# Down projections in another order of products, and the next norm's operands made step by step

## The chip, the cores and the metric

The kernel runs on one core of a Trainium2 chip. The metric is device time in microseconds, from launch to end, as the median of several runs. The kernel before takes 1988.11 us (three runs, 1987.03 to 1989.14). All times of single instructions come from one further, profiled execution.

## The reference

The reference is a decoder trunk of two layers on x of 512 tokens by 1024 channels, in float32. Each layer is

```
x += 1/2 * SwiGLU_1(RMSNorm(x))
x += W_out( g_pool * P_pool(PoolMixer) + g_attn * P_attn(SWA-GQA with sinks) )
x += 1/2 * SwiGLU_2(RMSNorm(x))
```

with

```python
def rmsnorm(x, g):
    y = xf * lax.rsqrt(jnp.mean(xf * xf, axis=-1, keepdims=True) + EPS)
    return y * g
def swiglu(h, w_gu, w_down):            # w_gu 1024 x 5632, w_down 2816 x 1024
    g, u = jnp.split(h @ w_gu, 2, axis=-1)
    return (jax.nn.silu(g) * u) @ w_down
```

The middle line, called mix below, has a pooling branch and a windowed attention branch on one norm. The change touches its end alone. There are four SwiGLU stages (called ffn), two mix stages, and the order is ffn, mix, ffn, ffn, mix, ffn.

## The kernel before

**Precision.** Every large matrix product is computed in three matmuls. An operand is split into a high part in fp32r, which ScalarE makes by a cast, and a low part, which VectorE makes by subtracting the high part from the operand (`split`, lines 148 to 161). Then high x high, high x low and low x high are added up in PSUM.

**Fewer products.** In an ffn, gate/up and down are done in the form of Strassen and Winograd: operand and weight are cut into 2 x 2 blocks, and seven products of sums of blocks take the place of eight. The seven products are named a11, s1, s2, a12, s3, s4 and a22. Each runs through `strassen` (line 526) as two chunks of weights, c = 0 and 1. A chunk is one tile of 128 x 1024 (smaller where the width is 384), and takes two quarters (q = 0 and 1) of six matmuls each: 24 matmuls a product. The results accumulate in pairs of PSUM banks, three of which have roles: a11, s2, s3 and a22 share pair A, s1 and s4 share pair C, and a12 has pair D. Within a pair the later product is added to the earlier one, so that between them an engine must have read the sum that is needed (`steps[kind]`), and the first matmul of the later product waits for that read. A and D change roles after each seven. A fourth pair, `turn`, takes transposes.

**Stages of an ffn.** The inner width of 2816 is done in three groups, of 2 x 384, 2 x 512 and 2 x 512 columns (the first ffn begins with the 384, the others have 512, 384, 512). A group is two `block` calls (gate and up for one half of its columns each, 384 or 512 wide) and one `down`, which multiplies the result with its rows of the down weights and adds it into x. After a block, `turned` transposes its results r and p with PE and makes operands of the down from them: the result t = 1 (p) at once, the result t = 0 (r) when `flush` is called later. `made` splits an operand into one of three tiles `op`, whose numbers are in AT (line 32): a name may reuse a tile only when the product that read it is done. f["a"], f["b"] and f["c"] are float tiles from which the operands s1, s2, a22, s3 and s4 come.

**Weights.** `Weights` holds a plan of all chunks in the order of use and a list of loads. A load goes by SP's DMA queue into one of seven raw tiles; where the chunk is a sum of two weight blocks (s1, s3), a second, accumulating DMA follows on POOL's queue. The chunks of s2 and s4 are not loaded: VectorE adds s2 from a11 and s1, and s4 from s2 and a12 (`add_up`). `prep` (line 288) is called once per chunk and looks ahead: low parts two chunks ahead, high parts three, sums four. A raw tile is free when its high part, its low part and its sum, if it has one, are made; only then is the next load issued. The sums lie in tiles of the pool `sums`, which is open only within an ffn (`open_sums`; W.sums is None outside).

**Order of the work.** All engines run in the order in which the program is written (`InOrder`, line 91, whose line 99 is the line that the profile shows for every instruction). Work beside the products is put in by hand: `steps` after a product, `mid` after a quarter of a product, and `pend`, a list of which `due` takes the first.

**The next norm.** While the last down of an ffn still adds into x, `feed(q, i, bank)` (line 374) transposes a part of x: token half i, channels of quarter q. ScalarE scales it by the norm's gain, and it is split. For a mix this is all. For an ffn (`halves`), feeds give the blocks B11, B12, B21 and B22, and combinations of them give the operands T1 = B11 - B12, T3 = B22 - B12, T2 (from B11 and T3) and T4 (from T2 and B21); j = 0, 1 are the two halves of each. Before, feed computes a combination as soon as its last block is there. The quarters (2, 0) and (3, 0) can only be fed after the last product's addition, and run in the next stage's first product. At the end of mix (lines 1118 to 1158) the same feeds run between the output products. `sums` of the norm (line 462) turns the sums of squares into rstd, in a chain of short VectorE instructions; the Silu after a12 needs it.

The order of products before is

```python
ORDER = ("a11", "s1", "s2", "a12", "s3", "s4", "a22")   # blocks
DOWN  = ("a11", "s1", "s2", "a12", "s4", "s3", "a22")   # downs
FIRST = ("a11", "s1", "a12", "s2", "s3", "s4", "a22")   # the first such block of an ffn
```

## Time and profile before

| what | value |
|---|---|
| median of three runs | 1988.11 us |
| the profiled execution: time | 1990.38 us |
| its span, first to last instruction | 1988.4 us |
| PE (TensorE) busy | 1885.0 us, 95% |
| DVE (VectorE) busy | 1453.1 us, 73% |
| ACT (ScalarE) busy | 1010.1 us, 51% |
| POOL (GpSimd) busy | 124.9 us, 6% |
| granted TensorE clock, mean | 0.989 |
| DMA | 292.80 MB, mean 147 GB/s |

The profile gives for each engine its busy time, for each instruction its start and length, and the idle time of its engine ahead of it with the engine and tile that ended it ("<-"). Tiles have the program's names: mm for PSUM pairs, wh and wl for high and low parts of weights, raw for loaded weights, sums for added ones, op for operands of a down, xgh, xgl and more for operands of a norm. A view of the timeline gives start, length, engine, line, operation, tiles and shapes, a count where equal instructions follow each other, and the wait in brackets. A view of stretches gives busy times between two moments.

### The profile page before, as it was taken

What the parts mean: (1) busy time and instruction counts of PE and PEld (TensorE: products, weight loads), DVE (VectorE), ACT (ScalarE), POOL (GpSimd) and SP (SyncE); (2) the same over time, 40 slices, a digit from 0 to 9 for tenths busy, and PEclk for the clock granted to TensorE, in tenths of its full rate; (3) what the DMA queues carried; (4) which work ended last, traced back from release to release, by engine and by line L of the source; (5) the groups of instructions that cost most, each with busy time, mean ns of one, the idle gap of its engine ahead of it and who ended that gap; (6) DMA issues with size and microseconds to landing.
All of it is one profiled execution on the core that took longest, in us unless ns stands there. A gap on an engine that the chain in (4) does not pass through costs nothing.

```text
span 1988.4 us, 23898 instructions
## 1 busy us (share of the span) xinstructions
PE 1885.0 (95%) x8928; PEld 1566.8 (79%) x8928; DVE 1453.1 (73%) x1829; ACT 1010.1 (51%) x1493; POOL 124.9 (6%) x152
## 2 busy tenths in 40 slices
PE   9999999899998899999879999998999998999998
PEld 8778787787787788878658797877877876889786
DVE  7877878567555787878767878785765647878777
ACT  6545455545435554545555454555454455545453
POOL 0100000000000000100000011000000000001100
PEclk9999999999999999999989999999999999999999
DMA  7776675322232766776546576753222236667763
GB/s 238 185 201 180 179 192 139 110 85 74 75 113 57 198 164 159 172 213 169 148 116 174 143 193 188 186 148 118 84 70 85 96 75 177 170 159 178 210 172 95
DMA packets 87571, 292.80 MB, mean 147 GB/s; under 512 B 9856, under 2 KB 10112, under 8 KB 87456
## 3 DMA queue, kind: packets, MB, share of 16 engines
q1 hardware_dynamic: 67104, 223.47, 33.8%
q0 software_dynamic: 20208, 67.78, 20.5%
q8 instruction: 70, 1.15, 0.2%
q14 instruction: 45, 0.37, 0.1%
q10 hardware_dynamic: 144, 0.03, 0.0%
HBM read 289.15 MB, written 2.10 MB: 146 GB/s over the span
## 4 chain that ended last, share of the span: by engine, by line
PE 71%; DVE 18%; ACT 6%; issue 3%; DMA 1%; SPq 0%; DVEq 0%; ACTq 0%; POOLq 0%
PE mm L99 65%; DVE wl L99 5%; DVE x L99 3%; PE sc L99 3%; DVE sums L99 2%; DVE op L99 2%; ACT wh L99 1%; DVE fa L99 1%; PE pt L99 1%; ACT xgh L99 1%; PE pt_pv L99 1%; DMA raw<-in_w_g 1%; ACT xg L99 1%; ACT more L99 1%; DVE t L99 1%
## 5 line engine op out<-in xcount | busy, mean ns | idle before, releaser
L99 ACT CAST wh<-raw 128x1024 fp32r<-128x1024 f32 (+3 forms) x443 | 434.2, 987 | 320.5 <-PE mm L99 244.8
L99 DVE TENSOR_TENSOR wl<-raw,wh 128x1024 fp32r<-128x1024 f32 (+3 forms) x443 | 505.6, 1145 | 119.9 <-PE mm L99 60.7
L99 PE MATMUL mm<-wh,op 128*128 128x512 f32 x1232 | 399.1, 399 | 35.5 <-DVE x L99 26.2
L99 PE MATMUL mm<-wh,more 128*128 128x512 f32 (+1 forms) x1104 | 338.0, 377 | 10.4 <-ACT u L99 10.4
L99 PE MATMUL mm<-wl,xgh 128*128 128x512 f32 (+2 forms) x840 | 312.9, 372 | 15.3 <-DVE wl L99 15.2
L99 PE MATMUL mm<-wh,xgh 128*128 128x512 f32 (+2 forms) x840 | 314.4, 374 | 0.1
L99 PE MATMUL mm<-wh,xgl 128*128 128x512 f32 (+2 forms) x840 | 311.5, 371 | 0.0
L99 PEld LDWEIGHTS mm<-wh,op 128*128 128x128 f32 x1232 | 233.3, 190 | 91.7 <-ACT wh L99 14.4
L99 PE MATMUL mm<-wl,op 128*128 128x512 f32 x616 | 245.8, 399 | 18.4 <-DVE wl L99 18.4
L99 PEld LDWEIGHTS mm<-wh,more 128*128 128x128 f32 x1104 | 208.0, 190 | 42.9 <-ACT u L99 12.0
L99 ACT CAST wh<-sums 128x1024 fp32r<-128x1024 f32 (+1 forms) x140 | 137.4, 982 | 161.7 <-DVE sums L99 142.7
L99 PE MATMUL mm<-wl,more 128*128 128x512 f32 (+1 forms) x552 | 208.5, 378 | 4.2 <-DVE wl L99 4.2
L99 PEld LDWEIGHTS mm<-wl,xgh 128*128 128x128 f32 x840 | 159.3, 190 | 40.6 <-DVE wl L99 19.6
L99 DVE TENSOR_TENSOR wl<-sums,wh 128x1024 fp32r<-128x1024 f32 (+1 forms) x140 | 156.7, 1135 | 41.8 <-ACT wh L99 22.0
L99 PEld LDWEIGHTS mm<-wh,xgl 128*128 128x128 f32 x840 | 159.3, 190 | 21.6
L99 PEld LDWEIGHTS mm<-wh,xgh 128*128 128x128 f32 x840 | 159.2, 189 | 21.4 <-ACT wh L99 0.4
L99 POOL DMA_DIRECT2D raw<-in_w_g x92 | 79.5, 864 | 1415.0 <-DMA raw<-in_w_g 662.9
L99 PEld LDWEIGHTS mm<-wl,op 128*128 128x128 f32 x616 | 117.3, 190 | 52.4 <-DVE wl L99 29.7
L99 PE MATMUL mm<-xgh,wh 128*128 128x512 f32 x320 | 129.5, 405 | 0.0
L99 PE MATMUL mm<-xgh,wl 128*128 128x512 f32 x320 | 125.2, 391 | 0.0
L99 PE MATMUL mm<-xgl,wh 128*128 128x512 f32 x320 | 125.0, 391 | 0.0
L99 DVE SCALAR_TENSOR_TENSOR x<-mm,x 128x1024 f32<-128x1024 f32 (+1 forms) x96 | 103.1, 1084 | 26.2 <-PE mm L99 26.2
(246 smaller groups left out, 2405.6 us busy)
## 6 DMA issues: line engine op xcount, KB each, us to landing
raw<-in_w_g SPq DMA_DIRECT2D x160, 512.0 KB, 4.5
raw<-in_w_d SPq DMA_DIRECT2D x100, 512.0 KB, 4.5
raw<-in_w_g POOLq DMA_DIRECT2D x64, 512.0 KB, 5.5
raw<-in_w_g SPq DMA_DIRECT2D x77, 384.0 KB, 3.9
raw<-in_w_d POOLq DMA_DIRECT2D x40, 512.0 KB, 5.5
raw<-in_w_gate SPq DMA_DIRECT2D x32, 512.0 KB, 3.3
raw<-in_w_g POOLq DMA_DIRECT2D x28, 384.0 KB, 5.1
raw<-in_w_br SPq DMA_DIRECT2D x16, 512.0 KB, 3.3
```

The costliest lines, as they stand in the source:

```text
L99: return lambda *args, **kw: self.tc.keep_in_program_order(call(*args, **kw))
```

## The change

- DOWN becomes a11, s1, s2, s4, s3, a12, a22, and the operand tiles get new numbers. f["b"] is finished after a11, the operand s4 is made after s1, s3 after s2, a12 in a flush after s4, and a22 after s3.
- FIRST goes away: the first block of an ffn uses ORDER. The order of the loads stays as it was in every block. The sums pool is opened at the start of each ffn but the first, not after a11. rstd is computed after s2, not after s1.
- The combinations become functions of their own: t1, t3 (only the float tile), t2, t3_split and t4. In the last down the feeds of token half 1 run in s3 and a12, those of half 0 in a22, where t3 and t1 also run. In mix, t1 follows its feed, and t3 stands after the last feed, ahead of the last additions into x.
- `left` puts on the list what remains: t2 twice, two feeds, t3_split twice, t4 twice. They run in a11 (t2 after its first quarter, the feeds after its second and third), s1 and s2 of the next ffn. For a mix only the two feeds are on the list.

```diff
-DOWN = ("a11", "s1", "s2", "a12", "s4", "s3", "a22")
-FIRST = ("a11", "s1", "a12", "s2", "s3", "s4", "a22")
+DOWN = ("a11", "s1", "s2", "s4", "s3", "a12", "a22")
...
-AT = {"a11": 0, "s1": 1, "s2": 2, "s3": 0, "a12": 1, "s4": 2, "a22": 1}
+AT = {"a11": 0, "s1": 1, "s2": 2, "s4": 0, "s3": 1, "a12": 2, "a22": 0}
...
-            head = [name[k, c] for k in (("a11", "s1") if order is FIRST else ("s1",)) for c in range(2)]
-            rest = [c for c in self.loads[first:] if not any(c is h for h in head)]
-            self.loads[first:] = head + rest
+            loads = ("a11", "s1") if start else ("s1", "a11")
+            self.loads[first:] = [name[k, c] for k in (*loads, "a12", "s3", "a22") for c in range(2)]
...
                 self.keep[1, j] = scaled(self.place(0, 0, j, F32))
-                d = temp("d")
-                nc.vector.tensor_tensor(out=d, in0=self.keep[0, j], in1=self.keep[1, j], op=ALU.subtract)
-                split(*self.both(T1, j), d)
-            elif i == 1:
-                xg = scaled(temp("xg"))
-                split(*self.both(B22, j), xg)
-                self.keep[2, j] = t = self.place(1, 0, j, F32)
-                nc.vector.tensor_tensor(out=t, in0=xg, in1=self.keep[1, j], op=ALU.subtract)
-                split(*self.both(T3, j), t)
             else:
-                xg, t, u = scaled(temp("xg")), temp("t2"), temp("t4")
-                split(*self.both(B21, j), xg)
-                nc.vector.scalar_tensor_tensor(
-                    out=t, in0=self.keep[0, j], scalar=-1.0, in1=self.keep[2, j], op0=ALU.mult, op1=ALU.subtract
-                )
-                split(*self.both(T2, j), t)
-                nc.vector.scalar_tensor_tensor(out=u, in0=t, scalar=-1.0, in1=xg, op0=ALU.mult, op1=ALU.subtract)
-                split(*self.both(T4, j), u)
+                self.keep[3 - i, j] = scaled(temp("xg"))
+                split(*self.both(B22 if i else B21, j), self.keep[3 - i, j])
+
+        def t1(self, j):
+            d = temp("d")
+            nc.vector.tensor_tensor(out=d, in0=self.keep[0, j], in1=self.keep[1, j], op=ALU.subtract)
+            split(*self.both(T1, j), d)
+
+        def t3(self, j):
+            self.keep[4, j] = t = self.place(1, 2, j, F32)
+            nc.vector.tensor_tensor(out=t, in0=self.keep[2, j], in1=self.keep[1, j], op=ALU.subtract)
+
+        def t2(self, j):
+            t = self.keep[0, j]
+            nc.vector.scalar_tensor_tensor(
+                out=t, in0=t, scalar=-1.0, in1=self.keep[4, j], op0=ALU.mult, op1=ALU.subtract
+            )
+            split(*self.both(T2, j), t)
+
+        def t3_split(self, j):
+            split(*self.both(T3, j), self.keep[4, j])
+
+        def t4(self, j):
+            u = temp("t4")
+            nc.vector.scalar_tensor_tensor(
+                out=u, in0=self.keep[0, j], scalar=-1.0, in1=self.keep[3, j], op0=ALU.mult, op1=ALU.subtract
+            )
+            split(*self.both(T4, j), u)
...
+    def left(nm):
+        last = [(lambda bank, q=q: nm.feed(q, 0, bank)) for q in (2, 3)]
+        if nm.halves:
+            step = lambda f: [(lambda bank, j=j: f(j)) for j in range(2)]
+            last = step(nm.t2) + last + step(nm.t3_split) + step(nm.t4)
+        pend.extend(last)
...
                 nc.scalar.copy(out=tile_["p"], in_=pt)
-                if nm.rstd is None:
-                    nm.sums()
...
                     nc.scalar.copy(out=tile_["u"][:, q, :], in_=pt[:, q, :])
+                if nm.rstd is None:
+                    nm.sums()
...
                 made("s2", f["a"], n)
-                nc.vector.tensor_tensor(out=f["b"], in0=f["c"], in1=f["b"], op=ALU.subtract)
...
-            a11 = add(0, 0, 0.5)
+            def a11(pt):
+                add(0, 0, 0.5)(pt)
+                nc.vector.tensor_tensor(out=f["b"], in0=f["c"], in1=f["b"], op=ALU.subtract)
 
             def s1(pt):
                 add(1, 1, -0.5)(pt)
-                made("s3", f["b"], n)
-                return flush
+                made("s4", f["c"], n)
 
             def s2(pt):
                 add(1, 0, 0.5)(pt)
-                made("s4", f["c"], n)
-
-            def a12(pt):
-                add(0, 0, 0.5)(pt)
-                made("a22", f["a"], n)
-                whole(0, 0)
-
-            def s3(pt):
-                add(1, 1, -0.5)(pt)
-                whole(1, 1)
+                made("s3", f["b"], n)
 
             def s4(pt):
                 add(1, 0, 0.5)(pt)
                 whole(1, 0)
                 if final:
                     W.sums = None
+                return flush
+
+            def s3(pt):
+                add(1, 1, -0.5)(pt)
+                made("a22", f["a"], n)
+                whole(1, 1)
+
+            def a12(pt):
+                add(0, 0, 0.5)(pt)
+                whole(0, 0)
...
-                Dd = roles[2]
-                for i, (kind, q, t) in enumerate((("s4", 0, 0), ("s3", 0, 1), ("a22", 2, 1))):
-                    for k in range(2):
-                        bank = (Dd, turn)[k][:, 0, :]
-                        mid[kind, k, 1] = lambda q=q + k, t=t, bank=bank: nxt.feed(q, t, bank)
-                pend.extend((lambda bank, q=q: nxt.feed(q, 0, bank)) for q in (2, 3))
+                spot = [t[:, 0, :] for t in (turn, roles[2])]
+                feed = lambda q, t, at: lambda: nxt.feed(q, t, spot[at])
+                mid.update({
+                    ("s3", 0, 1): feed(0, 1, 1), ("s3", 1, 1): feed(1, 1, 0), ("a12", 0, 1): feed(2, 1, 0),
+                    ("a12", 1, 1): feed(3, 1, 0), ("a22", 0, 1): feed(0, 0, 0), ("a22", 1, 0): feed(1, 0, 1),
+                })
+                if nxt.halves:
+                    mid["a22", 0, 0] = lambda: [nxt.t3(j) for j in range(2)]
+                    mid["a22", 1, 1] = lambda: [nxt.t1(j) for j in range(2)]
+                left(nxt)
...
+        if nm is not first:
+            open_sums()
...
-                    starts = W.sums is None
                     mid = {}
-                    if nm is first and starts:
-                        mid["s1", 1, 1] = flush
-                    elif starts:
-                        mid = {("a11", k, 1): lambda bank=bank: due(bank[:, 0, :]) for k, bank in ((0, turn), (1, roles[2]))}
-                    block(n, i, FIRST if starts else ORDER, mid)
+                    if nm is first:
+                        if gi == 0:
+                            mid["s1", 1, 1] = flush
+                    elif gi == i == 0:
+                        mid = {("a11", 0, 0): lambda: [due(), due()], ("a11", 0, 1): lambda: due(turn[:, 0, :]),
+                               ("a11", 1, 0): lambda: due(roles[2][:, 0, :])}
+                        mid.update({(kind, c, 1): due for kind in ("s1", "s2") for c in range(2)})
+                    block(n, i, ORDER, mid)
...
                     if d and b % 2:
-                        nxt.feed(*next(feeds), side_bank[b // 2])
+                        q, i = next(feeds)
+                        nxt.feed(q, i, side_bank[b // 2])
+                        if nxt.halves and i:
+                            nxt.t1(q)
...
                     nxt.feed(*next(feeds), side_bank[b])
+        for n in range(2):
+            nxt.t3(n)
         for n in (0, 1):
             added(1, n)
-        pend.extend((lambda bank, q=q: nxt.feed(q, 0, bank)) for q in (2, 3))
+        left(nxt)
```

More of the change, by code (lines that the diff above doesn't have):

```diff
@@ L189, in __init__ @@
                                 src = lambda h, k, c, w=w: w[h, 2 * k + c]
-                                self.block(src, (2 * n, 2 * n), FIRST if 2 * gi + i == int(plain) else ORDER)
+                                self.block(src, (2 * n, 2 * n), ORDER, 2 * gi + i == int(plain))
                         if at:
@@ L204, in add, with block @@
             return c
-        def block(self, w, sizes, order):
+        def block(self, w, sizes, order, start=False):
             name, first = {}, len(self.loads)
@@ L498, in trunk, with due @@
     pend = []
-    def due(bank):
+    def due(bank=None):
         if pend:
             pend.pop(0)(bank)
+    def left(nm):
[4 more added lines that the diff above has]
+        pend.extend(last)
     @with_exitstack
```

## The prediction

> **What bounds the kernel now.** I read the busy times and then PE's waits, because PE is busy 95% of the span and DVE 73%.
>
> ```profile
> PE 1885.0 (95%) x8928; PEld 1566.8 (79%) x8928; DVE 1453.1 (73%) x1829; ACT 1010.1 (51%) x1493; POOL 124.9 (6%) x152
> ...
> PE mm L99 <- DVE wl L99: 37.9, 38, 3.3
> PE mm L99 <- DVE x L99: 28.2, 14, 5.5
> PE mm L99 <- ACT u L99: 10.4, 4, 3.3
> PE mm L99 <- DVE op L99: 9.3, 12, 1.1
> PE pt L99 <- DVE x L99: 8.8, 6, 3.4
> ```
>
> Of the waits: total, count, longest. PE idles some 98 us in all. The second row is mostly a22 waiting until DVE has added s3 into x (same pair), the third s3 waiting for the copies of s2 in the first block of an ffn. The other three are PE waiting for VectorE work that stands in a queue. So I went through the stretches; the columns are length, busy time of PE, PEld, DVE, ACT, POOL, granted clock, DMA share, GB/s.
>
> ```profile
> 234.30:272.40 38.10, 38.10 (x171) 31.50 (x170) 27.34 (x25) 19.77 (x22) 2.81 (x4) 1.00 0.69 186
> 189.70:217.30 27.60, 25.50 (x119) 20.32 (x118) 26.41 (x25) 14.70 (x15) 2.58 (x3) 1.00 0.69 177
> 217.30:234.30 17.00, 15.59 (x69) 12.64 (x68) 11.67 (x11) 5.25 (x5) 0.87 (x1) 1.00 0.58 160
> 189.70:234.30 44.60, 41.09 (x186) 32.96 (x185) 38.08 (x34) 19.95 (x20) 3.45 (x4) 1.00 0.65 170
> 826.40:861.90 35.50, 31.35 (x140) 24.60 (x138) 31.39 (x34) 16.27 (x20) 4.02 (x5) 1.00 0.69 185
> 312.30:369.00 56.70, 49.18 (x226) 38.97 (x225) 43.72 (x43) 32.91 (x53) 1.86 (x3) 0.97 0.43 129
> 1310.20:1368.00 57.80, 50.21 (x227) 39.67 (x226) 43.82 (x43) 33.06 (x54) 1.86 (x3) 0.94 0.43 126
> 620.20:682.20 62.00, 50.19 (x211) 39.38 (x210) 41.49 (x57) 33.08 (x50) 3.45 (x4) 0.94 0.41 113
> 1619.00:1681.40 62.40, 51.95 (x211) 40.55 (x210) 41.49 (x57) 33.12 (x50) 3.45 (x4) 0.92 0.40 111
> 939.90:1052.50 112.60, 91.60 (x386) 72.25 (x385) 81.43 (x95) 58.85 (x88) 6.91 (x8) 0.92 0.49 131
> ```
>
> The first row is a gate/up block without a stall: seven products in 38.1 us, 5.44 each, 2.72 a chunk of twelve matmuls. The fourth is a down of width 512: the same seven products and two rounds of eight transposes (0.9 each) take 44.6, so 4.7 are lost. In its first part DVE is full (26.4 of 27.6), in its last third it is not (11.7 of 17.0). The fifth is a down of width 384. Then come final down to mix (twice), mix to ffn (twice) and final down to ffn, where time is lost and the clock drops.
>
> **The change, part by part. The downs.** There are nine without feeds: five of width 512 (the very last down is one) and four of 384. PE's rows of one, then DVE's:
>
> ```profile
> 190.37 0.47 PE L99 MATMUL mm<-wh,op 128*128 128x512 f32 x1
> 199.25 0.50 PE L99 MATMUL mm<-wl,op 128*128 128x512 f32 x1 [0.21 <-DVE wl L99]
> 201.89 1.04 PE L99 MATMUL pt<-cst,r 128*128 128x128 f32 x8
> 209.46 0.73 PE L99 MATMUL mm<-wh,op 128*128 128x512 f32 x2 [0.59 <-DVE op L99]
> 216.26 0.50 PE L99 MATMUL mm<-wl,op 128*128 128x512 f32 x1 [1.29 <-DVE wl L99]
> 228.62 0.47 PE L99 MATMUL mm<-wh,op 128*128 128x512 f32 x1 [1.41 <-DVE x L99]
> ```
>
> ```profile
> 196.85 1.22 DVE L99 TENSOR_TENSOR fb<-fc,fb 128x1024 f32<-128x1024 f32 x1
> 197.98 1.22 DVE L99 TENSOR_TENSOR wl<-raw,wh 128x1024 fp32r<-128x1024 f32 x1
> 201.39 2.35 DVE L99 TENSOR_TENSOR wl<-sums,wh 128x1024 fp32r<-128x1024 f32 x2
> 207.06 1.22 DVE L99 TENSOR_TENSOR sums<-sums,raw 128x1024 f32<-128x1024 f32 x1
> 227.25 1.23 DVE L99 SCALAR_TENSOR_TENSOR x<-mm,x 128x1024 f32<-128x1024 f32 x1 [1.67 <-PE mm L99]
> ```
>
> One step on DVE takes 1.135 us from start to start. The four waits sum to 3.5; the other 1.2 of the 4.7 is a restart of 0.3 after each. The a22 wait is no backlog: DVE was idle ahead of 227.25. I lay the new order on the same queue; no instruction is added or dropped.
> - fb leaves its place ahead of the low part (wl) at 197.98, which moves to 196.85: the wait of 0.21 goes. fb comes after the addition of a11, so the next low part, the first of s2, still starts at 201.39 and ends at 202.6. The transposes of r (201.89) had hidden that; they now come after s4. a11 and s1 end at 190.37 + 10.9 = 201.3, so s2's second matmul waits 1.1.
> - Behind it stand, 1.135 each: sum for s4 (it stood at 207.06, two products later), low part, sum, addition of s1, low part of operand s4, and then the low part of the first s4 weights, which ends at 209.4. s2 ends at 207.9, so s4 waits 1.35.
> - From there DVE gains: twelve steps to the low part of operand a22 end at about 223.5. PE: s4 ends at 214.7, transposes to 215.6, s3 to 221.0, a12 to 226.5, and a22 starts without a wait. The operand of a12 (218.4) is in time for 221.0.
> a22 then ends at 231.9 instead of 228.62 + 5.44 = 234.06. Two of four waits are left. I take 2.0 (the width 384 walks to the same within 0.2): 9 x 2.0 = **18 us**.
>
> **DMA.** The order of the loads stays. But a12's raw tiles are now freed by their low parts at about 217 and 221, where they were freed at 207 and 212 (sums at 207.06 and one step on), and of seven raw buffers these gate the next block's second s1 load and its first a11 load.
>
> ```profile
> raw<-in_w_g SPq DMA_DIRECT2D x160, 512.0 KB, 4.5
> raw<-in_w_g POOLq DMA_DIRECT2D x64, 512.0 KB, 5.5
> ```
>
> a11 is then issued near 221 and lands near 226 with 4.5, near 229 if it shares the engines with two others; the matmuls that read it start at 232. The s1 tile's second half, on POOL's queue, follows its first and is used 8 us later still. Cost nothing; at 384, where chunks are shorter, up to 0.5 after each of four downs. I book 0.
>
> **The boundaries.** PE's waits in the first ffn (one), from final down to ffn (four), and one each of mix to ffn and of final down to mix; then DVE's queue there and one row of ScalarE's:
>
> ```profile
> 63.46 0.44 PE L99 MATMUL mm<-wh,more 128*128 128x384 f32 x1 [0.95 <-ACT u L99]
> 976.66 0.63 PE L99 MATMUL mm<-cst,x 128*128 128x128 f32 x4 [1.03 <-DVE x L99]
> 985.95 0.80 PE L99 MATMUL mm<-wh,op 128*128 128x512 f32 x1 [5.48 <-DVE x L99]
> 1001.28 0.30 PE L99 MATMUL pt<-cst,x 128*128 128x128 f32 x1 [3.39 <-DVE x L99]
> 1033.03 0.79 PE L99 MATMUL mm<-wh,more 128*128 128x512 f32 x1 [3.33 <-ACT u L99]
> 631.84 0.30 PE L99 MATMUL pt<-cst,x 128*128 128x128 f32 x1 [2.38 <-DVE x L99]
> 356.90 0.79 PE L99 MATMUL mm<-wh,op 128*128 128x512 f32 x1 [4.03 <-DVE x L99]
> ```
>
> ```profile
> 979.59 0.69 DVE L99 TENSOR_TENSOR d<-more 128x512 f32<-128x512 f32 x1 [1.94 <-ACT more L99]
> 980.96 0.69 DVE L99 TENSOR_TENSOR xgl<-d,xgh 128x512 fp32r<-128x512 f32 x1 [0.68 <-ACT xgh L99]
> 984.68 1.22 DVE L99 SCALAR_TENSOR_TENSOR x<-mm,x 128x1024 f32<-128x1024 f32 x1
> 661.21 1.04 ACT L99 CAST wh<-raw 128x1024 fp32r<-128x1024 f32 x1 [1.93 <-DMA raw<-in_w_g]
> ```
>
> A combination costs DVE 2.05 us: 0.69, 0.68 of waiting for ScalarE's cast, 0.69. DVE runs in order, so the addition that a22 needs (984.68) stood behind two of them. I walk each boundary like the down.
> - **Final down to ffn.** Stall-free: 2 x 38.1, 1.8 of transposes for r and p, eight feeds of 0.6 (976.66): 82.8 of 112.6. After the change, counted from the last block's end: waits of 1.1 and 1.4 as above, 0.3 and 0.9 before feeds; a22 ends at 47.0. a11 starts at 48.6, 1.6 late: its pair is the old D, which holds the feed (1, 0) until ScalarE, behind two sums of squares and two casts, has scaled it. DVE has the low part of that feed at 49.9, then both T1, 4.1, then a22's additions, 1.2: 55.1, and the feed in a11, due at 51.3, waits 3.8. DVE goes on: a low part and a sum to 57.3, both T2 to 61.3, the feed's low part to 62.6, and to 63.8 the low part that s1 wants at 61.9: 1.9. Walked on, 1.8 and 0.2 in s3 and s4. In all 13.0. Restarts 9 x 0.3, and 1.5 for the clock after the 3.8: 100.0, 12.6 less. Counting restarts at the 0.13 that the walk of before needs gives 14; I take **13.3**.
> - **Mix to ffn**, twice. Stall-free 45.9 (38.1, two out tiles of 2.7, four feeds) of 62.2. T3's cast and low part leave the queue ahead of x, so 2.38 becomes 2.1 at most; then 0.3. From the additions' end, 11.4 after the start of the stretch, DVE has two low parts and a sum (4.2, with a wait for a cast), both T2 (4.0), the feed (1.4), and s1's low part ends at 22.1; s1 wants it at 18.6: 3.5. Then 0.2, 1.8, 0.2: 8.1. The waits for u go, and 661.21's too, because the sums are open from the start and free a11's raw tiles before a11 runs, not after. With restarts and 1 for the clock 56.4: 5.8 each, **11.6**.
> - **Final down to mix**, twice. 4.03 goes, but B11's counterpart comes later, so mix's first products wait 1.9 in all: 2.0 gained each, and the clock's loss, 1.5 and 2.6 (0.03 x 56.7 and 0.06 x 57.8, less what falls into the waits): **8.1**.
> - First block of the first ffn: its u wait is 0.95 and some returns as a wait for a12's low part: **0.5**. The 14 short instructions for rstd move to s2; Silu of a12, 5.4 us later, covers them.
>
> **The clock.** Where waits are short, as in 189.70:234.30, the granted clock stays 1.00; in the stretches with waits of 2.4 to 5.5 us it is 0.92 to 0.97. [...]
>
> **Sum.** 18 + 13.3 + 11.6 + 8.1 + 0.5 = 51.5 off the span of 1988.4: 1936.9. The profiled execution took 1990.38, 2.0 more than its span, and 2.3 more than the median of 1988.11; against the median that is **1936.6**.
>
> **Rivals.**
> - DVE takes it back: the waits at s2 and s4 grow to what the four were, and the later feeds are exposed. For it: DVE is full in 189.70:217.30, and the sums for s4 now stand in just that part. Against it: 5.3 idle DVE us follow in the last third. It loses the 18: **1955**.
> - More than the walk: no drop of the clock is left and the 3.8 and 3.5 shrink to about 1, as PE's own slips give DVE time. 2.8 + 2 x 2.5, the 3.5 booked for the clock, and half of the downs' two waits, 9 x 0.6: 16.7 more, **1920**.
> - Short waits trip the clock, one drop in each of 12 downs, 1.7 each (0.03 x 56.7, the one of 312.30:369.00): **1957**. The row with four waits at 1.00 speaks against it. [...]
> - Nothing gained: the pair was not what a22 waited for, and the moved feeds eat the rest: **1988**. The idle DVE at 227.25 speaks against.
> - Slower: the loads. a12's raw tiles are held 10 us longer in each of the 11 downs that have a successor. Between a11's usual landing at 226 and its use at 232 also lie its cast and low part, 2.3, which leaves 3.7. If the three loads and the accumulating one that are now issued together take over 8.2 us to land, PE stalls after each down, and from 4.7 us of stall on (a landing after 13) the gain is gone. At 5.5: **1997**. The DMA share of 0.65 in 189.70:234.30 speaks against.
>
> **Chances and range.** Forecast 0.50 (1926 to 1947), DVE takes it back or the feeds are exposed 0.22, more 0.14, clock 0.04, nothing 0.04, slower 0.06. From 1918 to 1960 lie about eight in ten. 0.2% is 4 us, what can be told from no change: faster 0.91, same 0.03, slower 0.06.
>
> **What would show it.** Right: no PE wait for DVE x at the start of a22, none for ACT u; two waits for wl of 1 to 1.5 in each down, at s2 and s4; downs of 42.5; the clock at 0.97 or more over the boundaries. Wrong: downs still at 44, ACT waiting for raw loads after a down, or a first product of an ffn that waits over 4 us.

## The result and the profile after

The changed kernel takes 1930.24 us (median of four runs, 1929.75 to 1930.87) where the kernel before took 1988.62 beside it: a ratio of 0.9708 [0.9691, 0.9724]. The forecast was 1936.6, with a range from 1918 to 1960. The profiled execution has a span of 1928.5 us, 59.9 less than the 1988.4 of before, and its mean granted clock is 0.997 (before 0.989).

The busy row of the page, then the first of PE's waits of the kernel after (in total, times, longest):

```profile
PE 1864.9 (97%) x8928; PEld 1558.4 (81%) x8928; DVE 1454.5 (75%) x1829; ACT 1009.1 (52%) x1493; POOL 124.3 (6%) x152
```

```profile
PE mm L98 <- DVE wl L98: 42.2, 34, 3.2
```

DVE does the same 1829 instructions in the same time. Three rows of before are gone: products waiting for x (28.2), for u (10.4) and for an operand (9.3). The waits for low parts of weights have grown from 37.9 to 42.2, those of transposes for x from 8.8 to 10.1. PE's busy time is 20.1 less although its 8928 instructions are the same. Much of that is the clock: its shortfall was 0.011 x 1988.4 = 21.9 us and is 0.003 x 1928.5 = 5.8.

The view of stretches, at the places that the prediction quoted, cut at the same events to within 0.2 us: a down of 512, one of 384, final down to mix (twice), mix to ffn (twice), final down to ffn. The columns are length, busy PE, PEld, DVE, ACT, POOL, clock, DMA share, GB/s.

```profile
186.76:229.51 42.75, 40.50 (x186) 33.13 (x185) 38.29 (x34) 20.18 (x20) 3.45 (x4) 1.00 0.65 171
807.86:841.28 33.42, 30.63 (x140) 24.76 (x138) 31.62 (x34) 16.25 (x20) 2.92 (x4) 1.00 0.73 195
307.45:360.40 52.95, 47.90 (x226) 37.59 (x225) 43.95 (x43) 32.90 (x54) 1.85 (x3) 1.00 0.48 139
1268.60:1321.60 53.00, 48.00 (x226) 37.65 (x225) 44.02 (x43) 32.98 (x54) 1.86 (x3) 1.00 0.46 138
611.60:665.50 53.90, 48.93 (x212) 38.63 (x211) 40.94 (x57) 32.54 (x50) 2.58 (x3) 0.97 0.47 128
1572.60:1627.35 54.75, 49.50 (x212) 39.71 (x211) 41.03 (x57) 33.01 (x50) 3.11 (x4) 0.94 0.47 126
919.30:1014.90 95.60, 84.61 (x387) 67.14 (x386) 81.19 (x95) 58.11 (x88) 6.68 (x8) 1.00 0.59 154
```

Beside the prediction's terms this gives, in us off the span:

| term | forecast | measured |
|---|---|---|
| nine downs without feeds | 18 | 5 x (44.60 - 42.75) + 4 x (35.50 - 33.42) = 17.6 |
| final down to ffn | 13.3 | 112.60 - 95.60 = 17.0 |
| mix to ffn, twice | 11.6 | (62.00 - 53.90) + (62.40 - 54.75) = 15.75 |
| final down to mix, twice | 8.1 | (56.70 - 52.95) + (57.80 - 53.00) = 8.55 |
| first block of the first ffn, and the rest | 0.5 | 1.0, what is left to 59.9 |

The timeline of PE in the kernel after, the rows that had to wait: one down of 512, mix to ffn twice, and final down to ffn.

```profile
199.73 0.50 PE L98 MATMUL mm<-wl,op 128*128 128x512 f32 x1 [0.93 <-DVE wl L98]
206.78 0.50 PE L98 MATMUL mm<-wl,op 128*128 128x512 f32 x1 [1.32 <-DVE wl L98]
...
622.44 0.30 PE L98 MATMUL pt<-cst,x 128*128 128x128 f32 x1 [1.45 <-DVE x L98]
633.54 0.50 PE L98 MATMUL mm<-wl,xgh 128*128 128x512 f32 x1 [1.66 <-DVE wl L98]
...
973.57 0.33 PE L98 MATMUL pt<-cst,x 128*128 128x128 f32 x1 [2.90 <-DVE x L98]
998.28 0.50 PE L98 MATMUL mm<-wl,more 128*128 128x512 f32 x1 [1.29 <-DVE wl L98]
...
1594.62 0.80 PE L98 MATMUL mm<-wl,xgh 128*128 128x512 f32 x1 [3.24 <-DVE wl L98]
```

The down has two waits, at s2 and at s4, and no other. All eight downs of 512 show the same two within 0.04, and the four of 384 show 1.43 to 1.44 and 1.31 to 1.36, so one of each width stands for the rest in the table. The timeline of DVE in the same down, and ahead of the feed at 973.57:

```profile
190.43 1.22 DVE L98 SCALAR_TENSOR_TENSOR fa<-fa,fc 128x1024 f32<-128x1024 f32 x1
192.77 1.22 DVE L98 TENSOR_TENSOR op<-fa,op 128x1024 fp32r<-128x1024 f32 x1 [1.12 <-ACT op L98]
...
197.32 1.22 DVE L98 TENSOR_TENSOR fb<-fc,fb 128x1024 f32<-128x1024 f32 x1
198.46 1.22 DVE L98 TENSOR_TENSOR wl<-sums,wh 128x1024 fp32r<-128x1024 f32 x1
...
205.51 2.35 DVE L98 TENSOR_TENSOR wl<-sums,wh 128x1024 fp32r<-128x1024 f32 x2
...
968.88 0.69 DVE L98 TENSOR_TENSOR d<-more 128x512 f32<-128x512 f32 x1
970.25 0.69 DVE L98 TENSOR_TENSOR xgl<-d,xgh 128x512 fp32r<-128x512 f32 x1 [0.69 <-ACT xgh L98]
972.23 0.69 DVE L98 TENSOR_TENSOR xgl<-d,xgh 128x512 fp32r<-128x512 f32 x1 [0.68 <-ACT xgh L98]
972.83 1.28 DVE L98 SCALAR_TENSOR_TENSOR x<-mm,x 128x512 f32<-128x512 f32 x2
```

The two low parts at 198.46 and 205.51 end the two waits: DVE goes from step to step without idling between 192.77 and them. Ahead of 192.77 it idles 1.12 for ScalarE's cast of operand s2, and in each T1 combination 0.69 and 0.68 in the same way.

### The profile page after: what moved, and what is told of

It reads as the page before. It is cut to its first block, busy times and chain, and to the rows that moved or that the text cites. A ratio compares the mean times of both kernels' runs of the same rounds, so it can differ in the third digit from the quotient of the medians.

```text
span 1928.5 us, 23971 instructions
## 1 busy us (share of the span) xinstructions
PE 1864.9 (97%) x8928; PEld 1558.4 (81%) x8928; DVE 1454.5 (75%) x1829; ACT 1009.1 (52%) x1493; POOL 124.3 (6%) x152
## 3 DMA queue, kind: packets, MB, share of 16 engines
q8 instruction: 70, 1.15, 0.2%
## 4 chain that ended last, share of the span: by engine, by line
PE 75%; DVE 16%; ACT 5%; issue 3%; DMA 0%; SPq 0%; DVEq 0%; ACTq 0%
PE mm L98 68%; DVE wl L98 5%; PE sc L98 4%; DVE sums L98 2%; DVE x L98 2%; PE pt L98 1%; DVE op L98 1%; PE pt_pv L98 1%; ACT wh L98 1%; DVE fa L98 1%; ACT op L98 1%; ACT xgh L98 1%; DVE more L98 1%; DVE fb L98 1%; ACT xg L98 1%
## 5 line engine op out<-in xcount | busy, mean ns | idle before, releaser
L98 PE MATMUL mm<-wh,op 128*128 128x512 f32 x1232 | 391.5, 393 | 0.0
L98 PE MATMUL mm<-wh,more 128*128 128x512 f32 (+1 forms) x1104 | 333.5, 373 | 0.0
L98 PEld LDWEIGHTS mm<-wh,xgl 128*128 128x128 f32 x840 | 158.8, 189 | 21.5
```

The costliest lines, as they stand in the source:

```text
L98: return lambda *args, **kw: self.tc.keep_in_program_order(call(*args, **kw))
```

## The experiments

The theory: the gain comes from three edits, each worth what it takes off a DVE queue that sets PE's waits, and what is left of a down is that queue's length. Rivals: one edit did all, or the waits are set by ScalarE, by loads or by the clock. All ratios are to the kernel before, run beside.

### s3 and a22 as neighbours again

```diff
-DOWN = ("a11", "s1", "s2", "s4", "s3", "a12", "a22")
+DOWN = ("a11", "s1", "s2", "s4", "a12", "s3", "a22")
```

The operands and feeds move with their products; the rest of the change stays.

> The changed kernel with one thing put back in the downs: s3 and a22 are neighbours again (a11, s1, s2, s4, a12, s3, a22), all operands still made one step at a time (a12 after s2, s3 after s4, a22 after a12). Theory pair: a22 waits for the addition of s3 again, 1.4 shown and 0.3 of restart in each of the nine downs without feeds, 15 us, and more in the three with feeds, where the addition stands behind the feeds' low parts, about 3 each: 24 us over the changed kernel, near 1954. Rival queue: what counted was the place of VectorE's steps, which are still spread out; then a22 starts without a wait and the time stays within 5 us of 1930.

Measured: 1942.35 us, ratio 0.9768 [0.9753, 0.9782], 12.1 more than the changed kernel. PE's timeline of a down in this kernel:

```profile
200.72 0.50 PE L98 MATMUL mm<-wl,op 128*128 128x512 f32 x1 [0.92 <-DVE wl L98]
207.77 0.50 PE L98 MATMUL mm<-wl,op 128*128 128x512 f32 x1 [0.42 <-DVE wl L98]
...
225.57 0.47 PE L98 MATMUL mm<-wh,op 128*128 128x512 f32 x1 [1.41 <-DVE x L98]
```

The wait of a22 for x is back at its old length, 1.41, so the shared pair made it, and the rival that it did not falls. Products wait 24.1 for x in this kernel, yet only 12.1 are lost: the waits for low parts fall from 42.2 to 31.3 (the one at s4 in this down from 1.32 to 0.42) and those of transposes for x from 10.1 to 5.0, while PE is busy 5.2 longer, with the mean clock at 0.994. The steps on DVE ahead of s4's low part are the same in both. What differs is PE's: with s3 and a22 as neighbours the transposes of r (0.9) run between s2 and s4 and cover the wait, and in the changed kernel they come after s4. This place is tried by itself further down.

### The first block in its old order

```diff
+FIRST = ("a11", "s1", "a12", "s2", "s3", "s4", "a22")
...
-                    block(n, i, ORDER, mid)
+                    block(n, i, FIRST if 2 * gi + i == int(nm is first) else ORDER, mid)
```

The weights' plan follows, and rstd is computed after s1 again.

> The changed kernel with the first block of each ffn in the old order again (a12 ahead of s2, s2 and s3 neighbours), rstd after s1, the combinations still one step at a time. Theory pair plus queue: s3 waits for ScalarE's copies of s2, which stand behind the casts of T4 and weights; a walk of the queues gives waits of 2.8 at s2 and 5.8 at s3 and 5.3 us more for each of three starts, under 1 for the first ffn, and one or two drops of the clock: 1946 to 1954. Rival: only the waits for u that the kernel before showed come back, 10.4 us and four restarts: 1942 at most.

Measured: 1954.54 us, ratio 0.983 [0.9815, 0.9845], 24.3 more. PE's timeline of this kernel after a mix:

```profile
655.21 0.79 PE L99 MATMUL mm<-wh,more 128*128 128x512 f32 x1 [5.88 <-ACT u L99]
```

Ahead of it, ScalarE's timeline:

```profile
653.57 0.62 ACT L99 CAST more<-t 128x512 fp32r<-128x512 f32 x1 [2.68 <-DVE t L99]
654.09 1.06 ACT L99 COPY u<-mm 128x512 f32<-128x512 f32 x2
```

Waits for u sum to 15.7 in this kernel, four of them; after the change there is none. In this order s3 follows s2 in the same pair, and ScalarE has to copy s2 out between them. Here that copy (654.09) stands on ScalarE's queue behind a cast for a late combination, which waits 2.68 for DVE. So with the combinations postponed, the removal of FIRST is the largest single part.

### The combinations at once, as before

```diff
                 self.keep[3 - i, j] = scaled(temp("xg"))
                 split(*self.both(B22 if i else B21, j), self.keep[3 - i, j])
+                if i:
+                    self.t3(j)
+                    self.t3_split(j)
+                else:
+                    self.t2(j)
+                    self.t4(j)
```

The steps on `pend` and T3 at the end of mix go; T1 follows its feed; the orders of products stay new.

> The changed kernel with the combinations made as soon as their blocks are there, as before, and not one step at a time: T3 whole behind each feed of B22, T1 behind each feed of B11 in the down, T2 and T4 behind each feed of B21. Orders of products as in the changed kernel. Theory queue: each combination's cast and low part stand on VectorE ahead of additions and low parts that PE wants; a walk gives 5.8 us more at final down to ffn and 2.0 at each of the two mix to ffn: 10 us over the changed kernel, 1940, and up to 5 more if the clock drops. Rival: the orders of the products alone make the gain, and this is within 3 us of 1930.

Measured: 1946.65 us, ratio 0.9789 [0.9773, 0.9806], 16.4 more, with the mean clock at 0.991. DVE's and PE's timelines at the final down to ffn:

```profile
962.78 0.68 DVE L98 TENSOR_TENSOR more<-xg,more 128x512 f32<-128x512 f32 x1
...
969.08 1.22 DVE L98 SCALAR_TENSOR_TENSOR x<-mm,x 128x1024 f32<-128x1024 f32 x1
970.44 1.09 PE L98 MATMUL pt<-cst,x 128*128 128x128 f32 x4 [4.49 <-DVE x L98]
```

The first feed in a22 waits 4.49 for x, where it waits 0.76 after the change (at 962.35 there), because DVE first does T3 and its split for both halves (962.78 to 969.08). The feed in a11, which waits 2.90 after the change, waits 0.93 here. At each of the three starts of an ffn a product also waits for ScalarE's copy of a11's result r, 8.3 us in all where the changed kernel has none: that copy stands behind the casts of T2 and T4. Undone alone, the three edits cost 12.1, 24.3 and 16.4; together 52.8 of the 58.4 between the medians. No one edit did all. That the sum comes so near the whole does not show that they are independent: the old first block waits 15.7 for u with the combinations postponed, and waited 10.4 before the change, with them made at once.

### One more step on DVE's queue in each down

```diff
                 nc.vector.tensor_tensor(out=f["b"], in0=f["c"], in1=f["b"], op=ALU.subtract)
+                nc.vector.tensor_tensor(out=f["a"], in0=f["a"], in1=f["a"], op=ALU.max)
```

The added instruction changes no value.

> The changed kernel with one more VectorE instruction in each of the 12 downs, an elementwise maximum of the f[a] tile with itself (128x1024 or 128x768, no change of the values), behind the addition of a11. Theory queue: VectorE bounds the first part of a down, so the wait at s2 grows by the whole instruction, 0.93 to 2.06, and the wait at s4 stays: 1.13 for eight downs of 512 and 0.9 for four of 384, 12.6 us, 1943; and since waits of 2.06 come near what made the clock drop in the changed kernel (2.0 idle within 3.4 us), some drops of 1.7, up to 20 us in all. Rival: VectorE has slack there and PE's waits are for something else; then nothing is lost.

Measured: 1942.11 us, ratio 0.9768 [0.9753, 0.9783], 11.9 more. PE's timeline of a down in this kernel:

```profile
201.52 0.50 PE L98 MATMUL mm<-wl,op 128*128 128x512 f32 x1 [2.06 <-DVE wl L98]
208.57 0.50 PE L98 MATMUL mm<-wl,op 128*128 128x512 f32 x1 [1.28 <-DVE wl L98]
```

The wait at s2 grew by 1.13 (0.93 to 2.06), just one step, in a down whose first part is full. ScalarE and the loads had the same work, so they don't set this wait. In the down at 320 us the clock drops to half right behind the longer wait, and in the whole span 27 waits for low parts are left of 34: likely a slower PE reaches s4 later and waits less there. So the waits for low parts grew by only 2.0 in all (42.2 to 44.2), and PE was busy 9.4 longer, with the mean clock at 0.991. That is taken up below.

### The subtraction fb in other places

It stands after a11 in the changed kernel. First back to its old place, behind operand s2:

```diff
                 made("s2", f["a"], n)
+                nc.vector.tensor_tensor(out=f["b"], in0=f["c"], in1=f["b"], op=ALU.subtract)
...
-                add(0, 0, 0.5)(pt)
-                nc.vector.tensor_tensor(out=f["b"], in0=f["c"], in1=f["b"], op=ALU.subtract)
```

> The changed kernel with the subtraction f[b] back at its old place, ahead of the low part of the second s1 weights. Theory queue: VectorE's work up to the first low part of s2 is the same, so that the wait at s2 is only cut in two (0.2 at s1 and 0.7 at s2), which costs at most a restart of 0.3 in each of 12 downs: 0 to 3.6 us more. Rival: that step's place was worth its whole length, 1.1 in each down: 13 us more.

Measured: 1929.84 us, ratio 0.9705 [0.9692, 0.9719]: no difference from the changed kernel. The wait is cut in two (0.25 at s1, 0.34 at s2 in a down of 512). Both places lie between 192.77 and the low part for s2, in the full part, and the low part comes at the same time. This part of the change was idle.

Then on GpSimd:

```diff
-                nc.vector.tensor_tensor(out=f["b"], in0=f["c"], in1=f["b"], op=ALU.subtract)
+                nc.gpsimd.tensor_tensor(out=f["b"], in0=f["c"], in1=f["b"], op=ALU.subtract)
```

> The changed kernel with the subtraction f[b] done by GpSimd, which is busy 6%, in place of VectorE. Theory queue: VectorE's queue is one step shorter where it is full, so the wait at s2 goes and that at s4 is 1.1 instead of 1.3: 1.1 less in eight downs and 0.9 in four, 12.5 us, and restarts of 0.3 where a wait goes altogether, 1914 to 1918. Rival port: GpSimd's work slows VectorE's instructions beside it (or comes too late for s3), and half or all of it is lost: 1924 to 1935.

Measured: 1953.67 us, ratio 0.9827 [0.9812, 0.9843], 23.4 more, worse than either expectation. All engines of a down in this kernel, in its timeline:

```profile
206.26 0.85 POOL L98 DMA_DIRECT2D raw<-in_w_g  x1 [7.62 <-ACT wh L98]
206.82 2.66 POOL L98 TENSOR_TENSOR fb<-fc,fb 128x1024 f32<-128x1024 f32 x1
207.06 4.64 DVE L98 TENSOR_TENSOR wl<-sums,wh 128x1024 fp32r<-128x1024 f32 x2
...
210.63 0.80 PE L98 MATMUL mm<-wl,op 128*128 128x512 f32 x1 [3.59 <-DVE wl L98]
```

Two things took the step's saving back, and a third came with them. GpSimd issues the accumulating loads, in order, and fb stood behind one that waited 7.62 us for its raw tile. And while fb ran, for 2.66 us, the two low parts on DVE took 4.64 where they take 2.35 after the change (205.51): 2.29 longer, about the 2.42 that fb still had to run at 207.06. What in GpSimd's step held DVE up is not shown. And the wait of 3.59 is followed by half clock: of the 21.5 that the span grew, 13.9 are busy PE, at a mean clock of 0.989.

Last, into the 1.12 us that DVE idles ahead of 192.77:

```diff
-                made("s2", f["a"], n)
+                made("s2", f["a"], n, lambda: nc.vector.tensor_tensor(
+                    out=f["b"], in0=f["c"], in1=f["b"], op=ALU.subtract))
```

The function given to `made` is called between the cast and the low part; the step after a11 goes.

> The subtraction fb moves into the 1.12 us in which VectorE idles at each down's start, between its combination fa and the low half of operand s2, while ScalarE makes the high half (192.77 in the trace of after). Same instructions, one other place. Queue theory: VectorE has a queue that is full from there to the down's last sum, and a step taken out of the full part and laid into idle time is worth up to its length, 1.13 us at 512 and 0.9 at 384: the wait of product s2 (0.93 at 512, 1.44 at 384) goes or falls to about 0.5, the one of s4 (1.3) falls by what is left. Per down 0.9 to 1.1, over nine downs without feeds 8 to 10 us, some more at the final ones: 1918 to 1922 against 1930.2. Rival: the waits stand because of the loads or of ScalarE's high halves, and the place of fb does not matter, as its old place after operand s2 did not: 1929 to 1931.

Measured: 1917.08 us, ratio 0.9642 [0.9629, 0.9656], 13.2 less than the changed kernel. The timeline of DVE in a down of this kernel:

```profile
189.62 1.22 DVE L98 SCALAR_TENSOR_TENSOR fa<-fa,fc 128x1024 f32<-128x1024 f32 x1
190.76 1.22 DVE L98 TENSOR_TENSOR fb<-fc,fb 128x1024 f32<-128x1024 f32 x1
191.96 1.23 DVE L98 TENSOR_TENSOR op<-fa,op 128x1024 fp32r<-128x1024 f32 x1
...
196.51 1.22 DVE L98 TENSOR_TENSOR wl<-sums,wh 128x1024 fp32r<-128x1024 f32 x1
```

The idle time is filled. From the combination fa to the low part for s2 it is 6.89 us (189.62 to 196.51) where it was 8.03 (190.43 to 198.46), one step less. The wait at s2 is gone at 512, and PE's waits for low parts fall from 42.2 to 31.0 in the span. It gained more than expected because nine downs were counted and the three final ones left open: all twelve have this wait (one of the final ones 0.90, in the trace after at 932 us), and at 384 it falls from 1.44 to 0.57. A down of 512 began its s4 1.15 earlier, 0.93 for the wait and 0.22 for its restart.

### The sums for s4 on GpSimd

```diff
-                    nc.vector.tensor_tensor(
+                    (nc.gpsimd if c["pool"] else nc.vector).tensor_tensor(
```

`pool` is set for the s4 sums of the downs.

> The changed kernel with the two sums for the s4 weights of each down (128x1024 or 128x768) done by GpSimd. Theory queue: two steps fewer on VectorE ahead of the low part that s4 waits for; if GpSimd takes up to 2.5 us for one, s2 waits no more, s4 less than 0.5, 2 us less in each down: about 1906. Rival: GpSimd's sum comes late, s4's high part waits for it on ScalarE, and the wait at s4 is 1.5 to 2 as before: no gain, 1925 to 1935.

Measured: 1991.37 us, ratio 1.0015 [1.0006, 1.0024], 61.1 more than the changed kernel, far worse than either expectation. The timeline of GpSimd and ScalarE in a down of this kernel:

```profile
210.10 0.85 POOL L98 DMA_DIRECT2D raw<-in_w_g  x1 [8.27 <-DMA raw<-in_w_g]
210.66 4.97 POOL L98 TENSOR_TENSOR sums<-sums,raw 128x1024 f32<-128x1024 f32 x2
213.36 1.05 ACT L98 CAST wh<-sums 128x1024 fp32r<-128x1024 f32 x1 [9.83 <-POOL sums L98]
```

A sum takes 2747 ns on GpSimd in the mean, 1.22 us on DVE. But the length is the smaller part. As with fb, the sums stand in GpSimd's order behind an accumulating load, which here waited 8.27 us for another load. ScalarE then waits for the sums, and products wait for the casts of operands that stand behind. These eight waits, 31.7 us in all and up to 5.0, are in the eight downs that have a successor in their ffn. In the four final downs the sums follow DVE's low part at once (at 333.69, for one), no product waits for an operand, and s4 waits 2.05 to 2.08 instead of 1.32. Moving these sums off the full engine lost all that the change had gained; of the 60.5 that the span grew, 27.0 are busy PE, at a mean clock of 0.980.

### T1 and T2 for both halves side by side, and with fb in its slot

A combination idles DVE for 0.68 to 0.69 us while ScalarE casts. Here the two halves j = 0 and 1 go side by side: both first steps, both casts, both low parts.

```diff
+        def two(self, src, i):
+            for j in range(2):
+                nc.scalar.copy(out=self.both(i, j)[0], in_=src[j])
+            for j in range(2):
+                hi, lo = self.both(i, j)
+                nc.vector.tensor_tensor(out=lo, in0=src[j], in1=hi.bitcast(F32), op=ALU.subtract)
...
-                    mid["a22", 1, 1] = lambda: [nxt.t1(j) for j in range(2)]
+                    mid["a22", 1, 1] = nxt.t1s
```

> The changed kernel with T1 (at the end of the final down to ffn) and T2 (in a11 of an ffn) made for both halves together: two combinations, two casts, two low parts, so that VectorE works on one half while ScalarE casts the other. Theory queue: each pair takes 2.75 us of VectorE's queue and not 4.1, as 0.68 of waiting goes twice. a22's additions come 1.4 earlier, so the feed in a11 waits 1.5 in place of 2.9; the low part in s1 comes 1.4 earlier at each of three starts: 2.05 to 0.7 or less, 1.66 to 0.3, 3.24 to 1.9. 5.5 us less, and up to two drops of the clock (1.7 each): 1921 to 1925. Rival: the low parts that s1 waits for are held by ScalarE's casts, not by the pair: no gain.

Measured: 1924.01 us, ratio 0.9675 [0.9662, 0.9688], 6.2 less than the changed kernel. The timeline of DVE ahead of the same feed:

```profile
967.56 1.29 DVE L98 TENSOR_TENSOR d<-more 128x512 f32<-128x512 f32 x2
...
970.14 1.28 DVE L98 SCALAR_TENSOR_TENSOR x<-mm,x 128x512 f32<-128x512 f32 x2
```

Both T1 now take 2.58 us (967.56 to 970.14) instead of 3.95 (968.88 to 972.83 in the trace after), and the feed waits 1.55 instead of 2.90. With fb between the cast and the low part as well:

> fb laid into VectorE's idle time at the down's start, and both token halves of T1 and of T2 made side by side (all first steps, all high halves, all low halves). The two shorten different stretches (downs; final down to next operand), so the queue theory expects the sum of the two alone: the 6.2 us of the second and the 8 to 12 of the first, 1912 to 1916. Rival: at the final downs both feed on the same waits, and the sum is 2 to 4 us short of that.

Measured: 1911.46 us, ratio 0.9612 [0.9599, 0.9625]. That is 18.8 less than the changed kernel; the two alone gave 13.2 and 6.2, 19.4. They add.

### The transposes of r between s2 and s4

```diff
                 made("s3", f["b"], n)
+                return flush
...
-                return flush
```

The flush after s4 is now after s2, with the operand of a12 that it makes.

> The eight transposes of r and the operand of a12 stand after s2 in place of after s4, as they do where s3 and a22 are neighbours; the order of products and all else stay as in the changed kernel. There the wait at s4 was 0.42 instead of 1.32 with the same steps on VectorE's queue ahead of its low part. Theory: the difference is TensorE's, 0.9 of transposes (0.7 at 384) that cover the wait. Then s4 waits 0.4 here too, and twelve downs gain 8 x 0.9 + 4 x 0.7 = 10 us: 1919 to 1923 against 1930.2. Rival: it returns one product later. The low part of the a12 operand and the combination fa, 2.27 us, now stand ahead of the second low part for s3, which by the queue ends at 214.6 on the clock of after and is wanted at 214.7; if it is late by as much as was gained, 1928 to 1931.

Measured: 1925.24 us, ratio 0.9682 [0.9668, 0.9695], 5.0 less than the changed kernel. PE's waits in this kernel:

```profile
PE mm L98 <- DVE wl L98: 32.8, 36, 3.2
PE mm L98 <- DVE x L98: 2.5, 3, 0.8
```

The waits for low parts fall by 9.4 (42.2 to 32.8), as the theory has it; the s4 wait of the down is 0.42. Of that, 3.7 went into later waits for x (products 2.5, transposes 11.3 where it was 10.1). They stand at feeds of final downs, not at s3 of each down, where the rival had them; that the two steps pulled forward on DVE cause them is likely, but was not tried. The last 0.7 was not traced. With all three edits together:

> The same place of the transposes, with fb in VectorE's idle time and both halves of T1 and of T2 side by side. There the s2 wait is gone and s4 waits 1.34, so the transposes have as much to cover. If the three edits add: 1911.5 less 9 to 10, 1901 to 1903. If the gain at s4 returns at s3: 1909 to 1912.

Measured: 1907.37 us, ratio 0.9591 [0.9578, 0.9604]: 4.1 less than with two edits and 22.9 less than the changed kernel. That lies between the two expectations: the wait at s4 fell (from 1.31 to 0.44 in a down of 512) and the waits for low parts with it, from 27.3 to 16.9, but as before 3.7 came back as waits for x, and PE was busy 1.3 longer. It is the fastest version of this study.

## Why the prediction was right, and where it was off

**The downs** were right by their own mechanism. The walk left the low part for s2 where it was and took away the transposes that had covered it: 201.39, or 198.45 on the clock of the trace after, where this down begins 2.94 earlier; it is at 198.46. Waits of 1.1 and 1.35 were walked, 0.93 and 1.32 came. a22 starts without a wait, and the term is 17.6 where 18 was booked. That the wait at s2 is DVE's queue is shown from both sides, by a step added and by a step taken out. The one at s4 is read off the trace: the low parts for s2 and s4 start 7.05 apart (198.46, 205.51), a product takes 5.44, and the rest of 1.6 is the wait of 1.32 and a restart. What the walk did not look for is an idle slot in the queue itself: the 1.12 ahead of 192.77, into which fb fits.

**Final down to ffn** was mis-sized, 13.3 booked and 17.0 measured; the mechanism was right. Of the 100.0 that the walk gave, 4.4 did not come. The waits sum to 11.0 (95.60 less the 84.61 of busy PE), not 13.0: they came at the places that were walked, but the feed's was 2.90, not 3.8, the one at s3 1.29, not 1.8, the 1.2 ahead of two earlier feeds was 0.76, and the 0.2 at s4 did not come. The 1.5 for the clock was not lost: the row of 919.30 has it at 1.00. That was luck: the edge of a window cut the wait of 2.90 into 1.79 and about 1.1 (last section). And what busy PE lies over the stall-free 82.8 is 1.8, not the 2.7 of nine restarts (13.3 was taken, between the two restart sizes, so 3.7 remain as the miss).

**Mix to ffn** was mis-sized in the same way, 11.6 booked and 15.75 measured. Waits of 8.1 were walked each time, and 4.97 and 5.25 came (length less busy PE), of which the first is 1.45 for x, not 2.1; the 1.8 walked for s3 was 1.30 the one time and nothing the other. The clock cost more than the 1 that was booked: busy PE is 48.9 and 49.5, where the walk had 48.3 with restarts and that 1. The low part that s1 waits for came where it was walked, 22.1 after the start of the stretch: the wait ends at 21.9 and 22.0. But the wait, walked as 3.5, is 1.66 the one time and 3.24 the other. At the first, the clock had dropped before it, so PE came later and waited less; at the second it dropped after it, and the s3 wait went in the same way. A slow clock and a wait ate the same time.

**Final down to mix** (8.1 and 8.55), **the first block** and **the loads** were as booked. The first block is 0.8 shorter (28.92 before and 28.08 after, between the transposes of p ahead of it and behind it): its wait of 0.95 for u is gone, and nothing came back for it. No product waits for a load after a down, and in ScalarE's timeline from 216 to 242 us none of its casts of raw tiles waits for a DMA. So the rival with the loads did not come up, nor did the one in which the pair was no cause (the old wait of 1.41 returned with the old order).

Of the signs that were named beforehand one failed: the clock is 0.94, not 0.97, over the second mix to ffn. The two terms that were off were both too small, so nothing cancelled: 6.4 of 58.4 were not foreseen.

**DVE takes it back** was the likeliest rival. It did not come, but it names what is left: the 0.93 and 1.32 that a down of 512 still waits are this queue's. Part of the 1.32 was there to be had: the walk put the transposes after s4 without asking what they would cover ahead of it. **Short waits trip the clock** did not come at 0.93 and 1.32, but in the kernel with the extra step half clock followed one wait of 2.06.

## What to carry to other kernels

Where an in-order engine is full for a stretch, walk its queue step by step and look for its idle slots first: the same instruction was worth nothing in two places of the full part, 13 us in a slot where the engine waited for another one's cast, and minus 23 on the idle engine. An idle engine is not a free one: its own order can hold a step behind a load that waits (7.62 us for fb, 8.27 for the sums). Two chains of the kind "A, then B, then A" belong side by side, both first steps ahead of both last ones (6.2 us here). When products are reordered to part two that share an accumulator, ask also which work of TensorE had covered another wait in the old order: here transposes of 0.9 us, without which s4 waited 1.32 and not 0.42.

## What was not expected of the hardware

**The clock's drops went by windows, not by single waits.** In the traces of before and after it falls to half for stretches of 3.41 us or twice that, which start on a fixed grid of that step within a run. Windows on that grid show how long PE idled in each. The view of stretches of the kernel after, two or three windows in a row at a time:

```profile
620.89:624.30 3.41, 1.40 (x7) 0.83 (x7) 3.14 (x5) 1.97 (x5) 0.00 (x0) 1.00 0.00 0
624.30:627.72 3.42, 3.42 (x11) 2.75 (x11) 2.96 (x3) 1.34 (x3) 0.00 (x0) 0.50 0.00 0
969.05:972.46 3.41, 1.62 (x8) 0.98 (x6) 2.04 (x4) 1.24 (x2) 0.00 (x0) 1.00 0.00 0
972.46:975.88 3.42, 2.04 (x10) 1.61 (x11) 3.42 (x5) 2.28 (x5) 0.00 (x0) 1.00 0.00 0
...
1590.28:1593.69 3.41, 1.10 (x5) 0.56 (x3) 2.03 (x4) 2.96 (x6) 0.86 (x1) 1.00 0.58 235
1593.69:1597.10 3.41, 2.48 (x6) 2.00 (x7) 3.41 (x4) 3.38 (x6) 0.00 (x0) 0.50 0.84 129
1597.10:1600.52 3.42, 3.42 (x10) 2.65 (x9) 3.40 (x5) 2.58 (x4) 0.00 (x0) 0.50 0.90 328
```

At 620.89 three waits of 1.45, 0.21 and 0.35 fall into one window, 2.01 idle of 3.41, and the next window has half the clock. The wait of 2.90 at 973.57 is cut by a window's edge at 972.46 into 1.79 and about 1.1, and no drop follows. The drop at 624.30 depends on where the grid falls as well: at the second mix to ffn the same three waits lie in two windows (1.37 and 0.63 idle), and no drop follows them. The wait of 3.24 lies mostly in one window (2.31 idle), and the next, at half clock, still idles 0.93, after which a third is at half clock too. In the kernel with the extra step:

```profile
320.32:323.73 3.41, 1.35 (x7) 0.81 (x6) 3.38 (x4) 0.00 (x0) 0.00 (x0) 1.00 0.94 276
323.73:327.14 3.41, 3.41 (x10) 2.66 (x9) 3.38 (x4) 2.15 (x3) 0.00 (x0) 0.50 0.33 133
```

In this down the s2 wait, grown to 2.06, is by itself followed by half clock (2.06 idle of 3.41), which the 0.93 of the changed kernel is not. Another window at full clock in this kernel, 1071.25 to 1074.66 with 1.92 idle, is followed by full clock. In the traces of before and after, of windows at full clock none with under 1.54 us idle was followed by half clock, all eleven with 2.0 or more were, and of the seven between one was (1.54; those of 1.58 to 1.83 were not). Of windows at half clock, all four with 0.65 or more idle were followed by another, and none of the twelve with 0.57 or less. That a window's sum decides is read off traces; no run varied the idle time alone, and what decides between 1.54 and 2.0 stays open. The clock is a large part of what the experiments lost: for the same 8928 instructions PE is busy 1864.9 after the change (mean clock 0.997), and 1873.4 with the old first block (0.992), 1874.4 with the combinations at once (0.991) and 1874.3 with the extra step (0.991), which is 8.5 to 9.5 of the 11.4 to 23.5 that their spans grew. The windows ahead of a drop were not idle throughout: 1.40 of 3.41 us were busy in the first row.

**A step on GpSimd held DVE up.** A step of 128 x 1024 takes 2.66 us (fb) or 2.75 (the mean of 20 sums) there against 1.22 on DVE, and DVE was held up for 2.29 of fb's. In that kernel the 104 low parts of this shape that DVE made from sums took 142.8 us in all, 126.3 after the change.
